# Products with the values in tied pairs of steps, and seven tiles for the weights, in a two-layer encoder

## The chip, the cores and the metric

The kernel runs on one core of a Trainium2 chip, in one launch. The metric is the device time of that core in microseconds (us). Five engines work in parallel, each through its own queue in order: TensorE (matmuls, PE in the profile, its weight loads PEld), VectorE (DVE), ScalarE (ACT), GpSimd (POOL) and SyncE (SP), which issues the transfers.

## The reference

An encoder of two layers over 1024 tokens of width 1024, all in float32:

```
layer 0: h += concat(MLA(u), stick_breaking(u)) @ w_out    u = rms_norm(h)
layer 1: h += band_attention(u) @ w_out                    u = rms_norm(h)
both:    h += (silu(u @ w_gate) * (u @ w_up)) @ w_down     u = rms_norm(h)
end:     rms_norm(h)
```

The two parts of layer 0's mixer, with 8 heads of 64 each, are what matters here:

```
stick:  z = q k^T / 8;  log_keep = log_sigmoid(-z) where s < t
        w = exp(log_sigmoid(z) + sum of log_keep over the keys between s and t)
        o = w @ v
latent: p = softmax(q k^T / sqrt(96), chunk-causal);  o = p @ v
```

## The kernel before, in words

Activations lie transposed, features on the 128 partitions and tokens along the row, in two halves of 512 queries. float32 products are made of three products of a high and a low part (`mm3`, lines 295 to 297); the products with the values (line 873) are taken in float32 as they are.

**Steps.** Heads are taken in four pairs. Stick-breaking goes, for each pair and query half, over blocks of 128 keys, from the last down to the first: 4 steps in the first half, 8 in the second, 48 in all. In the steps on the diagonal fewer query columns are alive (128, 256, 384, 512). A step (`sb_step`) has three parts. `scores` makes z for both heads (lines 942, 943), the minimum with a limit on VectorE (945, into a tile `zc` of the role "a"), exponential and logarithm on ScalarE, a maximum on VectorE (948), and splits the result into a high part (ScalarE) and a remainder, for head 0 on VectorE and for head 1 on GpSimd (both line 258). `weights` sums with a triangular matrix (964, 969) and adds the carry of the steps before (967), takes a new carry (ScalarE, and 972 on VectorE), subtracts (975) and takes the exponential, in place in `zc`. `outputs` makes the products with the values through `weighted`. Latent attention (`mla_attend`) has 48 steps too, from the first key block up: `scores` (1172 to 1174), the exponential into a tile of the role "a" (1175), sums of the exponentials on GpSimd or VectorE (1120), and `weighted`; after the last step of a half `soft_finish` makes the denominators (1137). The row maxima of the next half or pair (`mla_max`, 1097 on TensorE, 1099 on VectorE) go between the steps.

**Two heads side by side.** `weighted` issues two matmuls, one for each head, with 64 columns of weights each; they write the upper and the lower half of the same output tile. In the trace they are the ones with 128\*64, against 128\*128 of the others. `joined` binds an instruction to the one before it: it gets the highest priority and stands right behind it.

**Pipeline and order.** `step` keeps the parts of steps that are still to be issued. With `LAG` 2, a step's weights are issued two steps after its scores, its outputs two after that. `weave` puts projections of the next pair between the steps. The order on each engine is then made by a scheduling layer that works with priorities in program order and its own idea of when an instruction can start; only instructions tied by `joined`, and those of the feed-forward part, stand as written. Band attention (layer 1) ties its products with the values already by groups of four steps, with the argument `join` of `weighted` given by its own lag (`TOGETHER`).

**Tiles.** The mixer's temporaries come from `MIX0_TEMPS`: four tiles of 1024 columns for the role "a", three for "b", four for "c", three of 512 for "f". Scores and sums of both parts and the maxima share two double banks of PSUM (`banks`, tag "z").

Of the kernel before, what the change touches and what calls it, by code (L numbers as in the profile page):

```python
# [30 lines left out]
LAG = 2  # L31
TOP = 100000

TOGETHER = 4
G_MIX0, G_FFN0, G_MIX1, G_FFN1, G_FIN, G_CQ, G_CKV, G_N = 0, 8, 16, 24, 32, 40, 43, 45


MIX0_TEMPS = {"a": (4, 1024), "b": (3, 1024), "c": (4, 1024), "f": (3, 512)}
BAND_TEMPS = {"a": (6, 1024), "b": (2, 1024), "f": (2, 512), "bias": (3, 1280), "t": (2, 512), "y": (4, 512)}
FFN_TEMPS = {"vr": (4, 512), "vh": (3, 512), "vl": (3, 512), "s": (4, 512), "e": (8, 512), "x": (3, 512)}  # L40

# [118 lines left out]
class Trunk:  # L160
# [762 lines left out]
    def sb_step(self, p, hf, j, proj, vt, st, o_d):  # L923
        nc = self.nc
        mm = nc.tensor.matmul
        qq, kk, kl = proj
        kh, r = divmod(j, 4)
        ks = slice(r * P, (r + 1) * P)
        diag = kh == hf
        top = j == 4 * hf + 3  # L930
        c0 = r * P if diag else 0
        cs = slice(c0, HALF)
        x = {}

        def causal(t):
            nc.gpsimd.affine_select(out=t, in_=t, pattern=[[0, 2], [1, P]], compare_op=ALU.is_gt,
                                    fill=0.0, base=0, channel_multiplier=-1)

        def scores():
            z = self.banks()  # L940
            for e in range(2):
                mm(z[:, e, cs], kk[e][kh][:, ks], qq[e][hf][:, cs], start=True, stop=False)
                mm(z[:, e, cs], kl[kh][e][:, ks], qq[e][hf][:, cs], start=False, stop=True)
            zc, t = self.tmp("a"), self.tmp("b")
            nc.vector.tensor_scalar(zc[:, :, cs], z[:, :, cs], ZMAX, None, ALU.min)
            nc.scalar.activation(t[:, :, cs], zc[:, :, cs], AF.Exp)
            nc.scalar.activation(t[:, :, cs], t[:, :, cs], AF.Ln, bias=1.0)
            nc.vector.tensor_tensor(t[:, :, cs], t[:, :, cs], zc[:, :, cs], ALU.max)
            if diag:
                causal(t[:, :, c0:c0 + P])  # L950
            sh, sl = self.tmp("c", F32R), self.tmp("c", F32R)
            nc.scalar.copy(sh[:, :, cs], t[:, :, cs])
            for e in range(2):
                self.rest(("dve", "pool")[e], sl[:, e, cs], t[:, e, cs], sh[:, e, cs])
            x.update(zc=zc, sh=sh, sl=sl)

        def weights():
            if top:
                st["carry"] = self.tmp("b", F32R)
                nc.gpsimd.memset(st["carry"].bitcast(F32), 0.0)  # L960
            carry = st["carry"]
            b = self.banks()
            for e in range(2):
                mm(b[:, e, cs], self.tri, x["sh"][:, e, cs], start=True, stop=False)
            if not top:
                for e in range(2):
                    mm(b[:, e, cs], self.carry_ones, carry[:, e, cs], start=False, stop=False)
            for e in range(2):
                mm(b[:, e, cs], self.tri, x["sl"][:, e, cs], start=False, stop=True)
            if j > 0:  # L970
                nc.scalar.copy(carry[0:1, :, cs], b[0:1, :, cs])
                nc.vector.tensor_tensor(carry[32:33, :, cs], b[0:1, :, cs], carry[0:1, :, cs].bitcast(F32),
                                        ALU.subtract)
            w = x["zc"]
            nc.vector.tensor_tensor(w[:, :, cs], w[:, :, cs], b[:, :, cs], ALU.subtract)
            nc.scalar.activation(w[:, :, cs], w[:, :, cs], AF.Exp)
            if diag:
                causal(w[:, :, c0:c0 + P])

        def outputs():  # L980
            if top:
                st["o"] = self.out_bank()
                mm(st["o"], self.zeros, self.masks, start=True, stop=False)
            self.weighted(st["o"], vt, j, x["zc"], cs, False, j == 0)
            if j == 0:
                ot = self.tmp("f")
                nc.scalar.copy(ot, st["o"])
                nc.sync.dma_start(o_d[hf][4 + p], ot)

        idle = [lambda: None] * (LAG - 1)  # L990
        self.step(scores, *idle, weights, *idle, outputs)

# [106 lines left out]
        self.neg_max_rows(m2, hf + 1, [qs[e][hf][0][96:100, :] for e in range(2)])  # L1101
        yield

    def soft_step(self, lag, scores, cs, st, vt, j, first, last, dest):
        x = {}

        def front():
            ex = x["ex"] = self.tmp("a")
            scores(ex)
            if first:  # L1110
                st["ex"] = ex
            else:
                old = st["ex"]
                if "esum" not in st:
                    st["esum"] = self.tmp("b")
                    if cs.start:
                        self.nc.scalar.copy(st["esum"][:, :, 0:cs.start], old[:, :, 0:cs.start])
                else:
                    old = st["esum"]
                self.eng("dve" if dest[2] else "pool").tensor_tensor(st["esum"][:, :, cs], old[:, :, cs], ex[:, :, cs],  # L1120
                                                                     ALU.add)

        def back():
            if first:
                st["o"] = self.out_bank()
            self.weighted(st["o"], vt, j, x["ex"], cs, first, last)
            if last:
                self.soft_finish(st["o"], st["esum"], *dest)

        self.step(front, *[lambda: None] * (lag - 1), back)  # L1130
# [23 lines left out]
    def mla_attend(self, p, hf, proj, vt, o_d):  # L1154
        nc = self.nc
        mm = nc.tensor.matmul
        qs, ks = proj
        st = {}
        nj = 4 * hf + 4
        for j in range(nj):  # L1160
            kh, r = divmod(j, 4)
            bs = slice(r * P, (r + 1) * P)
            diag = kh == hf
            cs = slice(r * P if diag else 0, HALF)
            kr = 104 if diag else 100

            def scores(ex, kh=kh, bs=bs, cs=cs, kr=kr):
                z = self.banks()
                for e in range(2):
                    qh, ql = qs[e][hf]  # L1170
                    kth, ktl = ks[e][kh]
                    mm(z[:, e, cs], kth[0:kr, bs], qh[0:kr, cs], start=True, stop=False)  # L1172
                    mm(z[:, e, cs], kth[0:96, bs], ql[0:96, cs], start=False, stop=False)
                    mm(z[:, e, cs], ktl[0:96, bs], qh[0:96, cs], start=False, stop=True)
                nc.scalar.activation(ex[:, :, cs], z[:, :, cs], AF.Exp, scale=96 ** -0.5)

            self.soft_step(2 * LAG, scores, cs, st, vt, j, j == 0, j == nj - 1, (o_d[hf], p, p == 3))
            yield 1.0 if not diag else 1.0 - 0.25 * r


# [56 lines left out]
    def band_attend(self, p, hf, proj, tk, vt, o_d):  # L1237
# [5 lines left out]
        for n, j in enumerate(order):  # L1243
# [14 lines left out]

            self.soft_step(LAG + 1 + TOGETHER - 1 - n % TOGETHER, scores, cs, st, vt, j, n == 0, n == len(order) - 1, (o_d[hf], p, p == 7))
            yield 1.0 - 0.25 * (3 - i1 + i0)  # L1260
# [28 lines left out]
    def mixer0(self, h_d):  # L1289
# [4 lines left out]
        half = lambda hf, *e: self.out_half(hf, a["w_out0"], w_d, o_p[hf], lambda hf, m: a["x"][hf, m], ks, out, h_d, *e)  # L1294
        with self.phase("mix0", MIX0_TEMPS):
            self.load_consts()
# [250 lines left out]
```

## Time and profile before

| | |
|---|---|
| median of 3 runs | 2524.12 us (2521.48 to 2524.86) |
| profiled execution | 2524.37 us, its span 2521.8 us |
| TensorE matmuls | 2456.9 us busy, 97% of the span |
| TensorE weight loads | 1936.0 us, 77% |
| VectorE | 1849.5 us, 73% |
| ScalarE | 1156.1 us, 46% |
| GpSimd | 495.1 us, 20% |

The mean granted clock of TensorE is 0.994. Matmuls overlap in the records, so that TensorE's busy time is not its work: for what a product takes, the distance from one start to the next is read. The first mixer's attention lies between 73 and about 620 us, the band attention between about 1290 and 1820 us, the two feed-forward parts behind them.

### The profile page before, as it was taken

Reading aid. Unit: us, or ns where it says so; the run is one execution under the profiler, and the core shown is the slowest. Engines: PE = TensorE matmul, PEld = TensorE weight load, DVE = VectorE, ACT = ScalarE, POOL = GpSimd, SP = SyncE. Lnnn points to the kernel's source line nnn. Section 1 sums busy time; section 2 is a strip of 40 time slices with the busy share of each in tenths; the row PEclk is TensorE's granted clock in tenths of the full one; section 3 lists DMA queues with packets and bytes.
Section 4 is the critical chain, followed back from the end, with each engine's and each line's share of the span. In section 5 each row is a group of like instructions: output and inputs, shape, how many; then the busy total and the mean of one; then the engine's idle time right before and its main releaser. Section 6 shows DMA issues by size and latency. Waiting matters only on the chain.

```text
span 2521.8 us, 33700 instructions
## 1 busy us (share of the span) xinstructions
PE 2456.9 (97%) x11710; PEld 1936.0 (77%) x11710; DVE 1849.5 (73%) x3040; ACT 1156.1 (46%) x2004; POOL 495.1 (20%) x475
## 2 busy tenths in 40 slices
PE   8999989999999999999999999999999999999997
PEld 7766766667778888888888777776777888888886
DVE  6988897674886666677766777778688666667775
ACT  4777665444554444433253443434455444343324
POOL 0433325762000000000031334345200000000004
PEclk9999999999999999999999999999999999999998
DMA  4222102247444434576652222223853442447651
GB/s 152 58 63 62 46 21 62 61 138 234 173 140 140 146 107 145 167 260 219 207 180 70 80 88 76 76 92 124 263 174 135 145 145 102 150 160 262 219 207 71
DMA packets 192041, 341.73 MB, mean 136 GB/s; under 512 B 22400, under 2 KB 38656, under 8 KB 191872
## 3 DMA queue, kind: packets, MB, share of 16 engines
q1 hardware_dynamic: 191872, 339.59, 40.6%
q8 instruction: 92, 1.51, 0.2%
q14 instruction: 77, 0.63, 0.1%
HBM read 232.02 MB, written 92.80 MB: 129 GB/s over the span
## 4 chain that ended last, share of the span: by engine, by line
PE 74%; DVE 7%; DMA 2%; ACT 1%; issue 1%; POOL 0%; DVEq 0%; SPq 0%; POOLq 0%; ACTq 0%
PE z L77 25%; PE mm L77 14%; PE o L77 7%; PE mm L295 6%; PE mm L296 6%; PE mm L297 6%; PE o L873 3%; DVE u L77 2%; PE z L1253 1%; PE z L1254 1%; PE z L1227 1%; DVE u L318 1%; PE z L1172 1%; PE o L1137 1%; PE z L1097 1%
## 5 line engine op out<-in xcount | busy, mean ns | idle before, releaser
L77 PE MATMUL z<-u,wh 128*128 128x512 f32 x976 | 302.3, 390 | 6.4 <-DVE u L77 6.4
L77 PE MATMUL z<-u,vh 128*128 128x512 f32 x976 | 302.8, 392 | 1.9 <-DVE u L77 1.9
L295 PE MATMUL mm<-u,wh 128*128 128x512 f32 x720 | 287.6, 399 | 1.9 <-DVE f L1038 1.4
L296 PE MATMUL mm<-u,wh 128*128 128x512 f32 x720 | 283.4, 394 | 1.4 <-DVE u L258 1.4
L297 PE MATMUL mm<-u,wl 128*128 128x512 f32 x720 | 283.1, 393 | 0.0
L258 POOL TENSOR_TENSOR wl<-wr,wh 128x512 fp32r<-128x512 f32 (+2 forms) x95 | 122.5, 1293 | 775.7 <-ACT wh L253 710.4
L77 PE MATMUL mm<-u,wh 128*128 128x512 f32 x720 | 222.6, 390 | 0.0
L77 PEld LDWEIGHTS z<-u,wh 128*128 128x128 f32 x976 | 183.3, 188 | 47.3 <-DVE u L77 9.4
L77 PEld LDWEIGHTS z<-u,vh 128*128 128x128 f32 x976 | 183.7, 189 | 42.5 <-ACT u L77 2.9
L77 PE MATMUL z<-u,vl 128*128 128x512 f32 x488 | 190.4, 390 | 0.0
L77 PE MATMUL z<-u,wl 128*128 128x512 f32 x488 | 190.1, 390 | 0.0
L295 PEld LDWEIGHTS mm<-u,wh 128*128 128x128 f32 x720 | 135.3, 188 | 49.4 <-issue 22.5
L297 PEld LDWEIGHTS mm<-u,wl 128*128 128x128 f32 x720 | 135.4, 188 | 29.1 <-issue 1.7
L77 PEld LDWEIGHTS mm<-u,wh 128*128 128x128 f32 x720 | 135.2, 188 | 29.4 <-issue 1.0
L296 PEld LDWEIGHTS mm<-u,wh 128*128 128x128 f32 x720 | 135.5, 188 | 27.0 <-DVE u L258 2.0
L77 PE MATMUL mm<-u,vh 128*128 128x512 f32 x496 | 152.7, 389 | 0.0
L258 POOL TENSOR_TENSOR u<-wr,u 128x512 fp32r<-128x512 f32 x8 | 10.9, 1375 | 661.1 <-ACT u L253 661.1
L77 PE MATMUL mm<-u,wl 128*128 128x512 f32 x360 | 140.1, 389 | 0.0
L873 PE MATMUL o<-a,u 128*64 128x512 f32 (+3 forms) x768 | 139.2, 474 | 0.5 <-DVE f L1145 0.4
L1120 POOL TENSOR_TENSOR b<-b,a 128x512 f32<-128x512 f32 (+3 forms) x80 | 109.3, 1367 | 122.9 <-ACT a L1256 99.4
L77 ACT CAST wh<-wr 128x512 fp32r<-128x512 f32 (+1 forms) x190 | 110.5, 584 | 49.4 <-DVE wr L77 29.3
L77 ACT CAST vh<-vr 128x512 fp32r<-128x512 f32 (+1 forms) x166 | 95.9, 578 | 81.3 <-DVE vr L77 31.5
(244 smaller groups left out, 5815.7 us busy)
## 6 DMA issues: line engine op xcount, KB each, us to landing
u<-f_t SPq DMA_DIRECT2D x144, 256.0 KB, 5.0
vr<-in_w_up SPq DMA_DIRECT2D x88, 256.0 KB, 4.4
wr<-in_w_gate SPq DMA_DIRECT2D x88, 256.0 KB, 3.7
f_t<-x SPq DMA_DIRECT2D x72, 256.0 KB, 2.0
wr<-in_w_out SPq DMA_DIRECT2D x64, 256.0 KB, 4.0
f_t<-e SPq DMA_DIRECT2D x54, 256.0 KB, 3.5
ld<-f SPq DMA_DIRECT2D x54, 256.0 KB, 5.1
u<-u SPq DMA_DIRECT2D x96, 128.0 KB, 2.2
```

What stands on the lines that cost most here:

```text
L77: return lambda *a, **k: self.tc.keep_in_program_order(f(*a, **k))
L258: self.eng(eng).tensor_tensor(lo, src, hi.bitcast(F32), ALU.subtract)
L295: mm(out, wh, xh, start=first, stop=False, skip_group_check=onto)
L296: mm(out, wh, xl, start=False, stop=False, skip_group_check=onto)
L297: mm(out, wl, xh, start=False, stop=last, skip_group_check=onto)
L318: self.eng(eng).tensor_tensor(acc, acc, sq, ALU.add)
L873: return self.nc.tensor.matmul(o[rh, cs], vt[j // 4][:, j % 4, rh], w[:, e, cs], start=first, stop=last)
L1097: nc.tensor.matmul(z[:, e, :n], qs[e][hf][0][0:kr, r * P:(r + 1) * P], ks[e][kh][0][0:kr, :n], start=True, stop=True)
L1120: self.eng("dve" if dest[2] else "pool").tensor_tensor(st["esum"][:, :, cs], old[:, :, cs], ex[:, :, cs], ALU.add)
L1137: return nc.tensor.matmul(den[64 * e:64 * e + 64, :], self.ones[:, 0:64], esum[:, e, :], start=True, stop=True)
L1172: mm(z[:, e, cs], kth[0:kr, bs], qh[0:kr, cs], start=True, stop=False)
L1227: nc.tensor.matmul(z[:, e, :n], qs[e][hf][0][:, r * P:(r + 1) * P], ks[e][kh][0][:, k0:k0 + n], start=True, stop=True)
```

## The change

A constant `MLA_TOGETHER = 2` and an argument `join` for `soft_step`. In stick-breaking, the first step of each two issues its outputs one step later, together with the second's, and the second's product of head 0 is tied to the first's product of head 1. In latent attention the same is done for steps j and j + 1. The role "a" gets seven tiles in place of four, 12 KB more on each partition.

```diff
-MIX0_TEMPS = {"a": (4, 1024), "b": (3, 1024), "c": (4, 1024), "f": (3, 512)}
+MLA_TOGETHER = 2
+MIX0_TEMPS = {"a": (7, 1024), "b": (3, 1024), "c": (4, 1024), "f": (3, 512)}
...
+        second = (4 * hf + 3 - j) % 2 > 0
...
-            self.weighted(st["o"], vt, j, x["zc"], cs, False, j == 0)
+            self.weighted(st["o"], vt, j, x["zc"], cs, False, j == 0, second)
...
-        self.step(scores, *idle, weights, *idle, outputs)
+        self.step(scores, *idle, weights, *idle, *[lambda: None] * (not second), outputs)
...
-    def soft_step(self, lag, scores, cs, st, vt, j, first, last, dest):
+    def soft_step(self, lag, scores, cs, st, vt, j, first, last, dest, join=False):
...
-            self.weighted(st["o"], vt, j, x["ex"], cs, first, last)
+            self.weighted(st["o"], vt, j, x["ex"], cs, first, last, join)
...
-            self.soft_step(2 * LAG, scores, cs, st, vt, j, j == 0, j == nj - 1, (o_d[hf], p, p == 3))
+            self.soft_step(2 * LAG + MLA_TOGETHER - 1 - j % MLA_TOGETHER, scores, cs, st, vt, j, j == 0, j == nj - 1, (o_d[hf], p, p == 3), j % MLA_TOGETHER > 0)
```

Lines of the changed kernel behind the first edits stand two or three further down: 873 is 875 there, 948 is 951, 1097 is 1100.

On TensorE, at the start of stick-breaking, the kernel before has two products with the values (o), the sums (964 to 969), the next scores and three projection products between them:

```order
L873 MATMUL o_921<-a_768,u_575 64x128 x2
L964 MATMUL z_925<-c_849,masks 128x384 x2
L967 MATMUL z_925<-b_825,masks 128x384 x2
L969 MATMUL z_925<-c_850,masks 128x384 x2
L942 MATMUL z_937<-u_725,u_735 128x128
L943 MATMUL z_937<-u_725,u_737 128x128
L942 MATMUL z_937<-u_726,u_736 128x128
L943 MATMUL z_937<-u_726,u_738 128x128
L295 MATMUL mm_902<-u_587,wh_788 128x512
L296 MATMUL mm_902<-u_588,wh_788 128x512
L297 MATMUL mm_902<-u_587,wl_789 128x512
L873 MATMUL o_921<-a_804,u_575 64x256 x2
```

In the changed kernel the same two stand together, at the place of the second:

```order
L299 MATMUL mm_902<-u_587,wl_789 128x512
L986 MATMUL o_953<-masks 128x512
L875 MATMUL o_953<-a_768,u_575 64x128 x2
L875 MATMUL o_953<-a_804,u_575 64x256 x2
L297 MATMUL mm_902<-u_608,wh_788 128x512
L298 MATMUL mm_902<-u_609,wh_788 128x512
```

The first product moved behind the sums, the scores and the projections; one run of half-column matmuls is left of two.

On VectorE, in the second half of the first pair, the remainder for head 0 (c) was followed by the next step's full-width maximum (948); names carry their numbers here:

```order
L975 TENSOR_TENSOR a210_1191<-a210_1191,z241_1339 128x1024
L258 TENSOR_TENSOR c237_1296<-b235_1290,c236_1295 128x512
L948 TENSOR_TENSOR b244_1356<-b244_1356,a243_1355 128x1024
L255 CAST wh257_1444<-wr256_1442 128x512
L255 CAST wh303_1675<-wr302_1673 128x512
```

In the changed kernel the carry's remainder (975, 972 before) and the subtraction (978) stand between the two:

```order
L260 TENSOR_TENSOR c237_1294<-b235_1288,c236_1293 128x512
L975 TENSOR_TENSOR b181_1018<-z241_1339,b181_1018 1x1024
L978 TENSOR_TENSOR a210_1191<-a210_1191,z241_1339 128x1024
L951 TENSOR_TENSOR b244_1356<-b244_1356,a243_1355 128x1024
L260 TENSOR_TENSOR wl255_1437<-wr253_1434,wh254_1436 128x512
```

The remainder moved ahead of the carry and the subtraction, and the maximum behind both.

On TensorE in latent attention, second pair, second half, a product with the values stood between a maximum's scores (1097, z915) and the next step's scores (z917):

```order
L1174 MATMUL z914_4516<-u814_4105,u770_3914 128x256
L1097 MATMUL z915_4525<-u840_4214,u874_4346 128x384
L1097 MATMUL z915_4525<-u843_4222,u894_4432 128x384
L873 MATMUL o905_4479<-a900_4460,u699_3610 64x512 x2
L1172 MATMUL z917_4532<-u793_4013,u766_3905 128x128
```

In the changed kernel two projection products stand there:

```order
L1177 MATMUL z914_4514<-u814_4105,u770_3914 128x256
L1100 MATMUL z915_4523<-u840_4212,u874_4346 128x384
L1100 MATMUL z915_4523<-u843_4220,u894_4430 128x384
L297 MATMUL mm928_4574<-u647_3430,wh926_4570 128x512
L298 MATMUL mm928_4574<-u648_3431,wh926_4570 128x512
L1175 MATMUL z917_4532<-u792_4010,u766_3905 128x128
```

The product with the values moved one step ahead, to its partner; the projection products came forward.

## Rows read from the trace of the kernel before

**Rows 1.** The page, its first line.
```profile
span 2521.8 us, 33700 instructions
```

**Rows 2.** Busy time by stretch; columns in the first line.
```profile
core 0: us, PE busy (x) PEld busy (x) DVE busy (x) ACT busy (x) POOL busy (x), PEclk, DMA share, GB/s
73.00:95.00 22.00, 21.44 (x106) 14.85 (x105) 19.79 (x27) 15.52 (x25) 10.52 (x16) 1.00 0.28 75
95.00:146.00 51.00, 49.51 (x262) 35.79 (x261) 48.51 (x59) 38.55 (x55) 17.49 (x19) 1.00 0.19 54
146.00:167.00 21.00, 19.80 (x98) 14.08 (x99) 16.64 (x23) 14.08 (x23) 10.54 (x16) 1.00 0.23 61
167.00:218.00 51.00, 49.52 (x260) 35.97 (x260) 48.29 (x57) 38.19 (x54) 16.16 (x18) 1.00 0.22 60
239.00:302.00 63.00, 61.44 (x270) 43.45 (x271) 54.55 (x64) 41.81 (x54) 20.21 (x23) 1.00 0.20 58
302.00:334.00 32.00, 32.00 (x150) 23.88 (x149) 22.53 (x32) 20.33 (x32) 9.90 (x15) 1.00 0.10 32
334.00:360.00 26.00, 26.00 (x114) 19.54 (x115) 24.56 (x32) 18.34 (x26) 5.75 (x6) 1.00 0.07 20
360.00:386.00 26.00, 16.99 (x60) 11.01 (x57) 25.54 (x32) 14.44 (x24) 10.09 (x7) 0.80 0.11 33
...
420.00:620.00 200.00, 198.12 (x930) 130.88 (x929) 128.51 (x167) 87.14 (x136) 113.34 (x79) 1.00 0.39 125
```

**Rows 3.** TensorE in order of time, a lone step's products; start, length, instruction.
```profile
127.06 0.39 PE L297 MATMUL mm<-u,wl 128*128 128x512 f32 x1
127.38 1.08 PE L873 MATMUL o<-a,u 128*64 128x512 f32 x4
128.39 0.50 PE L295 MATMUL mm<-u,wh 128*128 128x512 f32 x1
128.72 0.39 PE L296 MATMUL mm<-u,wh 128*128 128x512 f32 x1
```

**Rows 4.** The same in band attention, four tied steps and the denominators.
```profile
1383.92 0.39 PE L297 MATMUL mm<-u,wl 128*128 128x512 f32 x1
...
1384.60 0.39 PE L297 MATMUL mm<-u,wl 128*128 128x512 f32 x1
1384.92 2.37 PE L873 MATMUL o<-a,u 128*64 128x512 f32 x16
1387.13 1.03 PE L1137 MATMUL o<-b,ones 128*64 128x512 f32 x4
1388.08 0.44 PE L1253 MATMUL z<-u,u 128*128 128x384 f32 x1
```

**Rows 5.** TensorE's waits in 73 to 330; total, times, longest.
```profile
PE z L969 <- POOL c L258: 3.0, 4, 1.1
...
PE z L969 <- DVE c L258: 0.8, 2, 0.5
```

**Rows 6.** VectorE's maxima (ns: shortest, median, longest) and one place in time.
```profile
L948 DVE TENSOR_TENSOR b<-b,a x45: 419/1212/2312, 77.0 to 392.2; 128x1024 f32<-128x1024 f32 x24, 128x256 f32<-128x256 f32 x7, 128x512 f32<-128x512 f32 x7, 128x768 f32<-128x768 f32 x7
...
195.66 0.69 DVE L258 TENSOR_TENSOR c<-b,c 128x512 fp32r<-128x512 f32 x1
196.27 2.31 DVE L948 TENSOR_TENSOR b<-b,a 128x1024 f32<-128x1024 f32 x1
```

**Rows 7.** Latent attention in order of time, from one step's scores to the next.
```profile
448.31 0.28 PE L1174 MATMUL z<-u,u 96*128 96x256 f32 x1
...
448.43 0.52 PE L1097 MATMUL z<-u,u 104*128 104x384 f32 x2
448.69 0.60 ACT L1175 ACTIVATE a<-z 128x512 f32<-128x512 f32 x1 [1.35 <-PE z L1174]
...
448.98 0.96 DVE L1099 TENSOR_REDUCE m<-z 128x2 f32<-128x768 f32 x1 [1.58 <-PE z L1097]
449.88 0.33 PE L1172 MATMUL z<-u,u 104*128 104x128 f32 x1
```

## The prediction

> **What bounds the kernel now.** I read the page first, for the span of 2521.8 us [rows 1]. Then the windows over the one stage that the change touches, the first mixer, 73 to about 620 us; the column to compare is TensorE's busy time against VectorE's [rows 2]. The stick-breaking part is eight stretches, one per head pair and query half. In the first halves (73 to 95, 146 to 167, 218 to 239, 302 to 334) TensorE is busy 19.8 to 32.0 us and VectorE clearly less, 16.64 to 22.53. In the second halves both are full: 49.51 and 48.51 us of 51 in 95 to 146, 49.52 and 48.29 in 167 to 218. From 334 to 386 VectorE has 24.56 of 26 and 25.54 of 26 us, and TensorE only 16.99 of 26 in the last stretch, at a granted clock of 0.80. In latent attention, 420 to 620, TensorE has 198.12 of 200 us and VectorE 128.51. So a shorter TensorE queue is worth its whole length in some stretches and little in others.
>
> **What a switch costs.** A product with the values is two matmuls that each use half of the array's columns (128*64), side by side. Alone in the stream of full products, such a pair of 512 columns takes from the product before it, at 127.06, to the second one after it, at 128.72: 1.66 us [rows 3]. Full products run at 0.227 us each (three from 1383.92 to 1384.60) [rows 4], so two of them are 0.45, and the lone pair costs 1.21. The band stage already ties such pairs: from 1384.92 to the first full product at 1388.08, four of 512, 384, 256 and 128 columns and the denominator's pair of 512 take 3.16 us [rows 4]. The lone one takes 1.01 over the same ends (127.38 to 128.39), so 1280 more columns cost 2.15 us, 1.68 ns a column, and a tied pair of 512 costs 0.86. Entering and leaving half-column work therefore costs 1.21 - 0.86 = 0.35 us, and that goes for each run that merges with its neighbour.
>
> **How many go.** Counted in the order of the two kernels, unbroken runs of half-column matmuls fall from 117 to 85. Stick-breaking has 48 steps, each a run of its own before; 29 runs now, not 24, since five of its pairs have other products between their two steps (so the tie isn't kept everywhere). The other 13 go in latent attention, where some denominators that followed their last product directly now stand alone; the count has that in it. 32 x 0.35 = 11.2 us, all on TensorE. No arithmetic goes or comes: each engine has as many instructions as before. From the last product with the values of latent attention on, TensorE's order is the same; nothing is expected there but the shift.
>
> **Where it lands, stretch by stretch.**
> First halves of stick-breaking: two runs fewer in each, 8 x 0.35 = 2.8 us. VectorE has 1.6 to 9.5 us less work than TensorE there. But the last product of the carry sum waits for GpSimd's half of the remainder, 3.0 us in four waits, longest 1.1 [rows 5]; in two of the four stretches TensorE arrives early and only waits longer. I take 2.4.
> Second halves: 4, 3, 2 and 2 runs fewer. Here VectorE must follow. Its work there is fixed, 48.51 us in 95 to 146, so the bounds are nothing and the full 0.35 a run. What tips it is the new order on VectorE. Its half of the remainder (0.69 us at 195.66) is followed at once by a full-width maximum with two SBUF inputs, and that one took 2.31 us, while the median of that line is 1.21 [rows 6]. Twice in the stage this stands so and costs 1.1 us, in 95 to 146 and in 167 to 218; in the new order the carry's remainder, with one input from PSUM, stands between them at both places. So VectorE gets some 1.1 us of room where it binds. I take 1.1 of 1.4, 0.9 of 1.05, 0.5 of 0.7, and in 334 to 386, where VectorE has under 2 us of idle time in 52 and TensorE waits for the latent norms, 0.2 of 0.7. Sum 2.7.
> The Trainium skill has a rule for this, in "SBUF — State Buffer", section "Who interferes with whom": a VectorE instruction with two SBUF inputs contends with a GpSimd instruction that reads SBUF, and the one that comes second is blocked, not slowed. The 2.31 us agree with that. By the rule the new order also pays where the remainder is now followed by another subtraction with two SBUF inputs (three places): 3.3 us at the same 1.1 each against 2.2 won, so the second halves would give about 1 us less.
> Latent attention: 13 x 0.35 = 4.55 us. Against it: two banks of scores alternate, and a lone product between two score groups used to give the exponential and the maximum time to empty them. In the row example the last score product starts at 448.31 and its exponential ends at 449.29 (448.69 + 0.60); the next scores can't start sooner in that bank, and before the product with the values kept TensorE busy to 449.88 [rows 7]. With the pairs, every second such gap holds two projection products in place of it: 448.43 + 2 x 0.17 + 2 x 0.227 = 449.23, 0.06 us short. The maximum of 768 elements ends at 449.94, just when TensorE would want its bank. Eight places like this at 0 to 0.25 us; I take 0.1, near what these rows give: 0.8 us lost, 3.75 left.
> The seven tiles: a weights tile of the pair's first step now lives five steps in place of four, and four tiles would have stopped the fifth step's minimum; with seven nothing waits for a tile. Before, the fourth tile was released by a product that stood ahead of the scores that need it, so it cost nothing then, and I give the two spare tiles nothing (bounds 0 to 1 us gained). The pair's first product now waits for the second's weights, and behind it on TensorE stand scores and projections; but the second product keeps its distance of four steps, so its weights are as old as before: 0, with 0.5 us lost as the other bound. The mixer's temporaries grow by 12 KB a partition and the feed-forward tiles lie over others: its first loads can wait for the last weights tiles. They overlay temporaries of the same stage before, too: 0 to 1 us, I take 0.
> Sum: 2.4 + 2.7 + 3.75 = 8.85 us. The profiled execution is 2524.37 us (its span 2521.8 and 2.6 around it), 0.25 over the median of the runs, 2524.12. 2524.37 - 8.85 = 2515.5 us.
>
> **Rivals.**
> All of it: 11.2 us, perhaps a little more with VectorE's 2.2; 2511 to 2513.2 us. For it: the second halves had TensorE fuller than VectorE, and the two collisions go. Against it: 334 to 386, where the chain of norms runs on VectorE.
> Stick-breaking pinned by VectorE: the queue there is remade by the scheduler, its work is the same, and TensorE's gain turns into waits for the remainder and the carry. Then only 302 to 334 (0.7, TensorE busy 32.00 of 32 us) and latent attention (3.75) are left, 4.45 us: 2519.9. For it: 48.51 of 51 us. "Perfetto Trace Analysis" in the Trainium skill, section "Identifying the Most-Contended Engine", says to judge VectorE by its occupancy and TensorE by its weight loads; by that rule VectorE (95%) and not TensorE (35.79 of 51 us, 70%) is the engine that binds in 95 to 146. Against it: 16.64 of 21 us in the first halves, and TensorE waited only 0.8 us for VectorE's half of the remainder in all of 73 to 330 [rows 5].
> Slower: the collision of the full-width maximum with GpSimd's half becomes the rule in place of the exception. There are 24 such maxima; 1.1 us each is 26 us, which with 8.85 saved gives 2542. It decides from eight new collisions on in the full stretches. For it: TensorE's earlier arrival moves the two engines against each other, and 2 of 24 collide already. Against it: the printed order puts another instruction between them more often than before.
>
> **How the numbers follow.** Forecast 0.52, its own range 2513 to 2519; all of it 0.20; pinned 0.23; slower 0.05. A difference of 0.2%, 5.05 us, is about what a measurement of this kernel can tell from none, so faster means under 2519.07. That holds all of the forecast and of the second case: 0.72; the pinned case is within it: 0.23; slower 0.05. The range, 2511 to 2521, takes in the full case, the pinned one and the bounds of the tiles and of the layout, and leaves out the slower one and part of the edges.
>
> **What would show it.** The half-column products of the first mixer in pairs, each pair of 512 columns with 0.86 us between its two starts, and 85 runs in the whole trace. The stage from the first product with the values to the last (73 to 620 us) shorter by 8 to 9 us, and everything behind it of the same length. No maximum of 2.31 us left on VectorE. Stretches 95 to 146 and 167 to 218 about 1 us shorter at VectorE's occupancy of 95% or more. In latent attention short new waits of scores for the exponential, under 0.25 us each. Wrong would be: TensorE's waits in 73 to 330 grown by some 5 us (pinned), a longer stretch at a clock of one half around 375 us, or a feed-forward stage that starts late.

## The result, and the profile after

The changed kernel takes 2528.75 us (median of 12 runs, 2525.29 to 2531.31), the kernel before 2523.34 in the same comparison (12 runs, 2519.27 to 2524.86): ratio 1.0021, 95% interval 1.0013 to 1.0028. It is 5.4 us slower; 8.85 us less had been forecast. The first line of its page answers to [rows 1]:

```profile
span 2528.6 us, 33696 instructions
```

The switches did go. On TensorE in order of time (start, length, instruction), two tied steps in the second half of the first head pair, which answers to [rows 3]:

```profile
126.16 0.44 PE L298 MATMUL mm<-u,wh 128*128 128x512 f32 x1
126.53 1.94 PE L875 MATMUL o<-a,u 128*64 128x512 f32 x8
128.40 0.50 PE L299 MATMUL mm<-u,wl 128*128 128x512 f32 x1
128.73 0.40 PE L297 MATMUL mm<-u,wh 128*128 128x512 f32 x1
```

From 126.16 to 128.73 is 2.57 us; less two full products at 0.227 that is 2.12 for both steps, against 2 x 1.21 = 2.42 for two lone ones: 0.30 us saved, near the 0.35 that was priced. The busy time by stretch (columns in the first line) answers to [rows 2]:

```profile
core 0: us, PE busy (x) PEld busy (x) DVE busy (x) ACT busy (x) POOL busy (x), PEclk, DMA share, GB/s
...
95.00:146.00 51.00, 47.55 (x259) 35.81 (x259) 48.16 (x56) 37.56 (x53) 17.38 (x19) 1.00 0.17 50
...
167.00:218.00 51.00, 47.14 (x249) 35.20 (x248) 45.80 (x52) 34.76 (x50) 14.95 (x18) 0.97 0.21 60
...
420.00:620.00 200.00, 195.64 (x924) 131.52 (x922) 130.58 (x165) 85.68 (x134) 114.76 (x80) 0.98 0.39 122
```

TensorE is idle where it was not: 3.45 us in 95 to 146 in place of 1.49, 3.86 in 167 to 218 in place of 1.48, 4.36 in 420 to 620 in place of 1.88, and in two of these stretches the granted clock is now below 1. The stretches are fixed in time, so they show where it idles, not how long a stage is. Its waits in 73 to 330 (total, times, longest) answer to [rows 5]:

```profile
PE z L967 <- DVE a L978: 4.4, 5, 2.0
PE z L972 <- DVE c L260: 3.3, 7, 0.8
PE z L972 <- POOL c L260: 2.6, 5, 1.1
PE o L875 <- POOL a L939: 1.4, 1, 1.4
```

With five smaller ones that is 13.7 us, against 7.2 before: 6.5 us more, where the prediction had named some 5 as a sign of being wrong. L967 is the first of the sums. It waits for L978, the subtraction on VectorE that empties the double bank of the sums of the step before; this wait was 1.3 us. L972, the last sum, waits for the remainders of both heads, 5.9 us where it was 3.8.

For the stages, distances between starts of TensorE's products were taken from the traces: stick-breaking from its first score product to step 48's, latent attention from its first score product to the last product with the values. "Tiles alone" below has the order of the kernel before. (Between the two stages lies a wait of TensorE that differs by 1 to 2 us from run to run of one order; it is left out of both.)

| kernel | half-column runs | stick-breaking, us | latent, us |
|---|---|---|---|
| tiles alone | 117 | 309.92 | 201.5 |
| changed kernel | 85 | +4.3 | +2.1 |
| stick-breaking alone | 98 | +3.2 | 0.0 |
| latent alone | 104 | -0.1 | +0.6 |
| stick-breaking's first halves | 109 | -0.6 | -1.3 |
| latent, pairs 1 and 2 | 111 | -0.1 | -2.3 |
| latent, chosen | 109 | -0.1 | -3.8 |
| three steps, untied | 116 | -0.4 | -3.0 |
| three steps, tied | 94 | -1.7 | -3.0 |
| three steps, latent chosen | 110 | -0.9 | -4.7 |

The two parts of the changed kernel are 6.4 us longer together; its profiled execution, 2530.52 us, is 7.7 above that of the tiles alone (2522.79). How far one execution can be trusted differs by stage. In stick-breaking the untied order repeats within 0.3 us (309.8 to 310.1). The tied order took 313.1 us twice and 314.2 in the changed kernel: the 1.1 us more lie behind one wait of 2.0 us at about 207 us, where in this execution alone the granted clock then stood at 0.50 for 3.4 us. The cost of the ties there is thus +3.2, not +4.3. In latent attention the first twelve steps differ by up to 1.4 us between executions of one order (the whole -1.3 of "stick-breaking's first halves" lies there, with the order of the tiles alone), and the changed kernel and "latent alone", which have one order there, differ by 1.5. So less than 1.5 us in the last column says nothing. By the executions without the extra half clock and with it, the two parts cost 3.8 to 5.3 us, of 5.4 between the medians.

### The profile page after: what moved, and what is told of

Same layout as the page of the kernel before. It is cut to its first block, busy times and chain, and to the rows that moved or that the text cites. A ratio compares the mean times of both kernels' runs of the same rounds, so it can differ in the third digit from the quotient of the medians.

```text
span 2528.6 us, 33696 instructions
## 1 busy us (share of the span) xinstructions
PE 2453.8 (97%) x11710; PEld 1941.6 (77%) x11710; DVE 1858.3 (73%) x3040; ACT 1155.7 (46%) x2004; POOL 497.0 (20%) x475
## 4 chain that ended last, share of the span: by engine, by line
PE 75%; DVE 7%; DMA 1%; issue 1%; ACT 1%; POOL 0%; DVEq 0%; SPq 0%; POOLq 0%; ACTq 0%
PE z L79 25%; PE mm L79 15%; PE o L79 7%; PE mm L297 6%; PE mm L298 6%; PE mm L299 6%; PE o L875 3%; PE z L1256 1%; DVE u L79 1%; PE z L1257 1%; PE z L1230 1%; DVE u L320 1%; PE z L1175 1%; PE o L1140 1%; PE z L1176 1%
## 5 line engine op out<-in xcount | busy, mean ns | idle before, releaser
L875 PE MATMUL o<-a,u 128*64 128x512 f32 (+3 forms) x768 | 133.6, 476 | 4.5 <-DVE f L1148 3.0
```

Source lines behind the costliest of these rows:

```text
L875: return self.nc.tensor.matmul(o[rh, cs], vt[j // 4][:, j % 4, rh], w[:, e, cs], start=first, stop=last)
```

## The experiments

Each was timed beside the kernel before; behind the ratio stands its 95% interval.

**The tiles by themselves.**

```diff
-MIX0_TEMPS = {"a": (4, 1024), "b": (3, 1024), "c": (4, 1024), "f": (3, 512)}
+MIX0_TEMPS = {"a": (7, 1024), "b": (3, 1024), "c": (4, 1024), "f": (3, 512)}
```

> The kernel before with seven tiles of the role a and nothing else; every engine's order is the same. Theory 1 (the loss comes from the new order alone): the time of before, within 1.5 us of 2523. Theory 2 (it comes from the larger temporaries, which lay the feed-forward tiles and the heap elsewhere): 2 to 5 us slower, and the stretch behind 620 us longer.

Measured: 2523.51 against 2524.02 us, ratio 0.9999 (0.9990 to 1.0007). The order on every engine is the same as before. The tiles and the layout cost nothing that can be told.

**Stick-breaking's ties alone, latent attention's alone.** From the changed kernel:

```diff
-MLA_TOGETHER = 2
+MLA_TOGETHER = 1
```

> Seven tiles, pairs tied in stick-breaking alone (98 half-column runs in place of 117). Theory 1 (its 19 removed switches, 6.7 us, come back as waits for the sums of the remade VectorE queue, and more): 1 to 3 us slower than before, with the stretch from 73 to 420 us longer by that. Theory 2 (the whole loss of the changed kernel is one blocked place in latent attention): 3 to 6 us faster. Theory 3 (pinned by VectorE): within 1 us.

Measured: 2528.06 us, 1.0012 (1.0004 to 1.0021). Nineteen switches went (6.7 us at 0.35), and stick-breaking became 3.2 us longer. Its waits in 73 to 301 are those of the changed kernel shown above within 0.2 us (4.5 for L978, 3.3 and 2.6 for the remainders). Those of the tiles alone in the same stretch:

```profile
PE z L969 <- POOL c L258: 2.8, 4, 1.1
PE z L964 <- DVE a L975: 1.3, 2, 0.7
PE z L942 <- DVE a L945: 1.2, 3, 0.4
PE z L967 <- DVE b L972: 0.9, 1, 0.9
PE z L969 <- DVE c L258: 0.8, 2, 0.5
```

The sums of all waits are 14.0 and 7.0 us. Over all of stick-breaking TensorE's idle time in the profile grew from 9.4 to 17.1 us: 7.7 more, less 6.7 of switches, is 1.0 of the 3.2. The other 2.2 would follow if the nineteen were worth 4.5 us in all, an estimate of 0.24 each, near the 0.26 of the band stage below. VectorE's busy time over the same steps grew from 271.8 to 276.0 us though its instructions are the same. Its remainders of projections (shortest, median, longest in ns; tiles alone, then stick-breaking alone):

```profile
L258 DVE TENSOR_TENSOR u<-u,u x18: 675/690/886, 72.7 to 255.2; 64x512 fp32r<-64x512 f32 x12, 128x512 fp32r<-128x512 f32 x6
```

```profile
L260 DVE TENSOR_TENSOR u<-u,u x18: 675/692/1784, 73.3 to 252.5; 64x512 fp32r<-64x512 f32 x12, 128x512 fp32r<-128x512 f32 x6
```

The median stays, single ones take 1.78 us. The collision with GpSimd went from the maximum to other instructions. The longest wait for L978 shows both what stands in front of it and such a collision (TensorE, then VectorE, start, length, instruction; stick-breaking alone):

```profile
201.27 0.73 PE L972 MATMUL z<-c,masks 128*128 128x512 f32 x2
...
207.41 0.70 PE L967 MATMUL z<-c,masks 128*128 128x512 f32 x2 [2.00 <-DVE a L978]
```

```profile
201.14 1.84 DVE L257 CAST wh<-wr 128x512 fp32r<-128x512 f32 x2
202.91 0.68 DVE L260 TENSOR_TENSOR wl<-wr,wh 128x512 fp32r<-128x512 f32 x1
203.51 0.68 DVE L260 TENSOR_TENSOR c<-b,c 128x512 fp32r<-128x512 f32 x1
204.11 0.68 DVE L260 TENSOR_TENSOR wl<-wr,wh 128x512 fp32r<-128x512 f32 x1
204.82 1.21 DVE L975 TENSOR_TENSOR b<-z,b 1x1024 fp32r<-1x1024 f32 x1
206.05 1.22 DVE L978 TENSOR_TENSOR a<-a,z 128x1024 f32<-128x1024 f32 x1
```

The sums end at 202.0. VectorE then has no pause, but it does two casts (the first 1.50 us, beside a subtraction of GpSimd), the remainders of two weights, the remainder of another step and that of the carry before it subtracts, and TensorE waits for the bank. The bank is late because other work stands ahead of its release in VectorE's queue.

Latent attention's ties alone, again from the changed kernel:

```diff
-        second = (4 * hf + 3 - j) % 2 > 0
+        second = True
...
-            self.weighted(st["o"], vt, j, x["zc"], cs, False, j == 0, second)
+            self.weighted(st["o"], vt, j, x["zc"], cs, False, j == 0)
```

> Seven tiles, pairs tied in latent attention alone (104 runs). Theory 1: up to the last first half of queries 3 to 4 us are gained; if VectorE's subtraction for the output loads is again blocked behind GpSimd's at the flush of that half (one of 3 us in place of 0.7, TensorE idle some 3 us, a stretch at half clock), 2 to 3 us slower than before in sum, and if not, 3 us faster. Theory 2 (latent ties gain nothing anywhere): the time of before without such a block.

Measured: 2523.40 us, 0.9997 (0.9988 to 1.0006). Thirteen switches went, and the stage is 0.6 us longer. By blocks of 12 steps the distances are +0.2, -1.4, +0.4 and +1.3 us. The loss sits at one place, where the third head pair hands over to the fourth: counted from the stage's first scores, those of step 40 come 2.3 us earlier than with the tiles alone, and those of step 41 come 2.2 us later. In the changed kernel, which has the same order in this stage, the place is at about 546 us. It does this on VectorE and on GpSimd (start, length, instruction):

```profile
542.97 4.70 DVE L260 TENSOR_TENSOR u<-ld,u 128x512 fp32r<-128x512 f32 x2
547.70 0.70 DVE L1147 SCALAR_TENSOR_TENSOR o<-o,f 128x512 f32<-128x512 f32 x1
548.31 0.76 DVE L1123 TENSOR_TENSOR b<-b,a 128x256 f32<-128x256 f32 x1
549.00 0.68 DVE L1148 SCALAR_TENSOR_TENSOR f<-o,f 128x512 f32<-128x512 f32 x1
```

```profile
542.42 1.76 POOL L260 TENSOR_TENSOR u<-c,u 96x512 fp32r<-96x512 f32 x1 [1.00 <-ACT u L255]
544.14 1.30 POOL L260 TENSOR_TENSOR u<-ld,u 128x512 fp32r<-128x512 f32 x1
545.82 1.31 POOL L260 TENSOR_TENSOR u<-ld,u 128x512 fp32r<-128x512 f32 x1 [0.37 <-ACT u L255]
```

Two remainders (the splits of the loaded stick-breaking outputs) last 4.70 us together, beside three subtractions of GpSimd; in the kernel before the two at this place took 1.48 and 1.16 us. Behind them stand the divisions of `soft_finish` (1147, 1148), which free the output bank. TensorE needs that bank for the four products of the next half:

```profile
546.38 0.39 PE L299 MATMUL mm<-u,wl 128*128 128x512 f32 x1
549.73 4.54 PE L875 MATMUL o<-a,u 128*64 128x512 f32 x16 [2.96 <-DVE f L1148]
554.05 1.69 PE L1140 MATMUL o<-b,ones 128*64 128x512 f32 x4
```

It waits 2.96 us, and during the wait, at 548.6, the granted clock is halved for 6.8 us (PEclk, the third number from the end, is 0.50, so 1.2 GHz):

```profile
548.60:555.40 6.80, 5.67 (x20) 2.14 (x20) 3.68 (x6) 0.00 (x0) 0.20 (x1) 0.50 0.61 207
```

The same block in the kernel before:

```profile
546.68 2.37 PE L873 MATMUL o<-a,u 128*64 128x512 f32 x16 [0.39 <-DVE f L1145]
548.85 1.06 PE L1137 MATMUL o<-b,ones 128*64 128x512 f32 x4
```

It took 2.37 us after a wait of 0.39; now it takes 4.54 after 2.96. With latent attention's ties alone the wait is 2.96 us too, the half clock lasts 3.4 us and the block takes 3.70: with the denominators behind it, that is the 1.5 us between the two runs in this stage.

**Moving the splits off that place.** In the changed kernel, the splits of the loads on VectorE alone:

```diff
-                self.split(t, hi, lo, "act", "pool" if k % 2 else "dve")
+                self.split(t, hi, lo, "act", "pool" if k % 2 and self.temps is not MIX0_TEMPS else "dve")
```

> The changed kernel with the first mixer's output loads split on VectorE alone, none on GpSimd. Theory 1 (the blocked subtraction at about 543 us costs TensorE 3 us of idle time and then 3 us at half clock): the wait of the four tied products at about 547 us falls under 1 us and the time is 4 to 6 us below the changed kernel, some 2523. Theory 2 (the lock is incidental, the denominator's chain is late anyway): within 1 us of the changed kernel, 2528.

Measured: 2529.71 us, 1.0027 (1.0018 to 1.0035): a miss. The 3.0 us for L1148 became 1.9, but a new wait of 3.0 us (scores for an exponential) and a new stretch at half clock (575 to 582 us) came in the last eight steps, and the latent stage is 4.3 us longer than with the tiles alone. The opposite, with ties in latent attention alone and both splits on GpSimd:

```diff
-                self.split(t, hi, lo, "act", "pool" if k % 2 else "dve")
+                self.split(t, hi, lo, "act", "pool" if k % 2 or self.temps is MIX0_TEMPS else "dve")
```

> As the run with ties in latent attention alone, but with the output loads of this mixer split on GpSimd alone, so that no such subtraction stands on VectorE ahead of the denominator's chain. Theory 1 (the subtraction that was blocked for 3 us delayed that chain): the wait of the four products for the last multiplication falls from 3.0 us to under 1, no half clock behind it, and the time is 3 to 5 us below that run, some 3 us below before. Theory 2 (the chain is late for other reasons): within 1 us of that run.

Measured: 2521.27 us against 2524.57, 0.9988 (0.9979 to 0.9996). The wait for L1148 is gone, and the stage is 2.2 us shorter than with the tiles alone, 2.8 shorter than with the same ties and the old splits. That fits the splits having held it, as do the 1.9 us that stayed with all of them on VectorE. But in both runs the scheduler remade the order of every engine around that place, so the splits are not the only thing that changed.

**Ties in latent pairs 1 and 2 only.**

```diff
+            tied = MLA_TOGETHER if p < 2 else 1
-            self.soft_step(2 * LAG + MLA_TOGETHER - 1 - j % MLA_TOGETHER, scores, cs, st, vt, j, j == 0, j == nj - 1, (o_d[hf], p, p == 3), j % MLA_TOGETHER > 0)
+            self.soft_step(2 * LAG + tied - 1 - j % tied, scores, cs, st, vt, j, j == 0, j == nj - 1, (o_d[hf], p, p == 3), j % tied > 0)
```

> Seven tiles, pairs tied in latent attention for the first two head pairs alone (111 runs). Theory 1 (the ties gain 0.35 us a run less some tenths, and the loss is one place at the change from the third head pair to the fourth): 1.5 to 2 us faster than before, no wait of 3 us at about 546 us. Theory 2 (the new waits for the exponentials and maxima take all): the time of before.

Measured: 2519.35 us, 0.9982 (0.9973 to 0.9991). Six runs fewer, 2.1 us at 0.35, and the stage is 2.3 us shorter. Its steps 13 to 36 are 2.5 us shorter, and 2.5 to 2.6 in each later run that has these ties. All of TensorE's waits in 420 to 620:

```profile
PE mm L298 <- DVE u L260: 1.2, 1, 1.2
PE o L875 <- DVE f L1147: 0.4, 1, 0.4
```

**Stick-breaking's first halves only.** Latent attention untied, and:

```diff
-            self.weighted(st["o"], vt, j, x["zc"], cs, False, j == 0, second)
+            self.weighted(st["o"], vt, j, x["zc"], cs, False, j == 0, second and hf == 0)
...
-        self.step(scores, *idle, weights, *idle, *[lambda: None] * (not second), outputs)
+        self.step(scores, *idle, weights, *idle, *[lambda: None] * (not second and hf == 0), outputs)
```

> Seven tiles, pairs tied in the first query halves of stick-breaking alone (109 half-column runs in place of 117). Theory 1 (in the second halves VectorE binds, and its remade queue brings subtractions and casts that stand blocked beside GpSimd; the first halves have room): 2 to 3 us faster than before, the second halves as long as before. Theory 2 (any remaking of the order costs more than the switches give): 1 us slower or more.

Measured: 2523.32 us, 0.9997 (0.9988 to 1.0007). Stick-breaking is 0.6 us shorter, of 2.8 for eight switches. The four first halves are 3.1 us shorter (0.84, 1.20, 0.77 and 0.27) and the second halves, whose code is that of before, 2.4 us longer; but part of both is work that moved: of each pair five matmuls (two steps' products with the values and the one that clears their bank) now start behind the boundary between the halves.

**Is the price of a switch real where the ties already stood?** The kernel before, with band attention tied by twos:

```diff
-TOGETHER = 4
+TOGETHER = 2
```

> The kernel before with band attention tied by two steps in place of four: 141 half-column runs in place of 117, all 24 in the band stage, with the same arithmetic. The price of a switch by itself: at 0.35 us each, 8.4 us slower (7 to 10) if TensorE binds there throughout; under 3 us if most of a switch hides in waits there.

Measured: 2524.42 us, 0.9997 (0.9988 to 1.0007), with 55 runs in band attention in place of 31. Its waits in 1290 to 1790, of the kernel before and of this one:

```profile
PE z L1253 <- DVE a L1255: 7.3, 6, 1.2
PE z L1227 <- DVE m L1230: 2.3, 4, 1.0
```

```profile
PE z L1253 <- DVE a L1255: 1.2, 6, 0.2
PE z L1227 <- DVE m L1230: 1.1, 2, 0.7
```

24 more switches are 8.4 us by the price above, and the stage is as long: from the first product of line 1253 to the last 450.51 us, against 450.17 and 450.52 in two executions of the order before (the kernel before and the tiles alone). The same six waits of scores for the bank emptied on VectorE shrink from 1.2 to 0.2 us each. TensorE's idle time between those products falls from 10.6 to 4.3 us, 0.26 a switch: a switch does cost TensorE time, somewhat less than 0.35 here, and is paid out of waits.

**Is it VectorE's load?** The kernel before with both heads' remainders on GpSimd, and the same with stick-breaking's ties and seven tiles:

```diff
-                self.rest(("dve", "pool")[e], sl[:, e, cs], t[:, e, cs], sh[:, e, cs])
+                self.rest("pool", sl[:, e, cs], t[:, e, cs], sh[:, e, cs])
```

> The kernel before with both heads' remainders in stick-breaking on GpSimd (head 0's moves off VectorE: some 40 subtractions, 30 us less on VectorE between 73 and 373 us, 60 more on GpSimd). It is the base for the next run. If VectorE binds the second halves, these get shorter, by 1 us or more each; if the step's own chain binds, they get longer, since the remainders come later.

> The same with pairs tied in stick-breaking (95 half-column runs in place of 117) and seven tiles. Theory 1 (the ties' gain was lost because VectorE, at 95% and with new blocked instructions, could not follow): with VectorE relieved the ties pay, 4 to 7 us faster than the run before this one. Theory 2 (a lone product was cover for the step's chain of scores, exponential, logarithm and remainder, whichever engine is loaded): no faster than that run, within 2 us or slower.

Measured: 2530.28 us, 1.0023 (1.0014 to 1.0033), and 2526.98, 1.0012 (1.0001 to 1.0022), both against 2524.61. VectorE is relieved to 183.85 of 227 us in 73 to 300 untied and 180.52 tied (203.38 with the tiles alone). Waits in 73 to 301, untied, then tied:

```profile
PE z L969 <- POOL c L258: 11.6, 15, 1.3
```

```profile
PE z L972 <- POOL c L260: 11.8, 18, 1.7
PE z L967 <- DVE a L978: 2.2, 4, 0.6
PE z L970 <- DVE b L975: 2.2, 2, 1.1
```

Stick-breaking takes 316.35 us untied and 315.33 tied: 22 switches (7.7 us) bring 1.0 us, with VectorE at 81% and 80%. So relieving VectorE doesn't bring the gain; but GpSimd's half became a new wait of the same kind, so this alone doesn't tell what held the gain back before.

**Is it the distance from scores to weights?** One more step between them in stick-breaking, with tiles that fit (a 6, b 3, c 6, f 2), untied and tied:

```diff
-        self.step(scores, *idle, weights, *idle, outputs)
+        self.step(scores, *idle, lambda: None, weights, *idle, outputs)
```

```diff
+        self.step(scores, *idle, lambda: None, weights, *idle, *[lambda: None] * (not second), outputs)
```

> The kernel before with one more step between a stick-breaking step's scores and its weights (three in place of two), six tiles for the role a, six for c, two for f; products with the values one by one (48 lone runs in stick-breaking). If the step's own chain (minimum, exponential, logarithm, maximum, split, remainder) sets the second halves, the added step gives it room: TensorE's waits in stick-breaking fall from about 14 us to under 8, and stick-breaking's 48 steps take 304 to 308 us in place of 309.9. If VectorE's queue sets them (272 of 310 us busy, and blocked behind GpSimd), the depth changes nothing: 309 to 311 us.

> The same with stick-breaking's products with the values tied by pairs (26 runs in place of 48, 22 x 0.35 = 7.7 us of switches less). If a lone product was only cover for a chain that came too late, the chain has room now and the ties pay: 5 to 7 us less in stick-breaking than without them at the same depth. If VectorE's queue binds, they pay 0 to 1 us, as with both remainders on GpSimd.

Measured: 2518.97 us, 0.9981 (0.9972 to 0.9989), and 2522.03, 0.9990 (0.9982 to 0.9999), both against 2523.90. Waits in 73 to 301, untied, then tied:

```profile
PE z L967 <- DVE a L978: 6.2, 7, 1.7
PE o L875 <- POOL a L939: 1.5, 1, 1.5
PE z L945 <- DVE a L978: 1.2, 1, 1.2
PE z L970 <- DVE b L975: 0.7, 2, 0.5
```

```profile
PE z L967 <- DVE a L978: 10.6, 10, 2.0
PE z L970 <- DVE b L975: 2.4, 3, 1.7
PE z L967 <- DVE a L948: 1.4, 2, 1.2
PE z L945 <- DVE a L948: 1.2, 3, 0.6
```

The waits for a remainder (3.6 us with the tiles alone, 5.9 with ties) are gone altogether: the added step does cover the chain of exponential, logarithm, split and remainder. Stick-breaking is hardly shorter for it (309.49 us), and 22 ties bring 1.25 us, not the 5 to 7 of the first theory. What is left, and grows with the ties from 9.0 to 15.6 us, are waits for VectorE to empty a double bank (L978, L948) and to make the carry (L975). They go from one step's sums to the next step's, and a step added between scores and weights gives that way no more time: sums, carry on ScalarE, its remainder on VectorE, subtraction on VectorE, bank free. But most of the time on it goes to other work. In the tied kernel 1.3 to 6.3 us lie between the end of the sums and the start of the subtraction in the ten waits for L978, 41 us together; in nine of them VectorE does work of other steps or of projections there, some 27 us. Before the wait that ends at 168.84 the sums end at 163.2 and the subtraction starts at 168.0, and VectorE does not pause: a maximum of 1.23 us, two remainders of projections (0.68 and 0.80), the carry's remainder (0.68) and the remainder of another step, which takes 1.72 us beside GpSimd's. This is read from the trace; no run put the subtraction further ahead in the queue. Collisions alone don't explain it: from untied to tied VectorE's busy time over these steps grows by only 0.6 us (273.7 to 274.3), and still 6.4 of 7.7 us are lost. One thing stays open: by the two stages the tied kernel should be 1.3 us faster than the untied one, and its median is 3.1 us slower. In the two profiled executions (2519.66 and 2520.15 us) the passage between the two stages is 2.0 us longer in the tied one, but it differs by that much between runs of one order.

**Versions that beat both.** Ties in latent pairs 1 and 2 and the second half of pair 4; the same with stick-breaking's first halves; the same with the untied three steps. Against the two latent pairs:

```diff
-            tied = MLA_TOGETHER if p < 2 else 1
+            tied = MLA_TOGETHER if p < 2 or p == 3 and hf else 1
```

> Ties in latent attention where the earlier runs gained: the first two head pairs and the last half of the fourth; none in stick-breaking (109 runs). By the stretches of the earlier runs, 2.3 us from the first two pairs and 1.6 from the last half: 3 to 4.5 us faster than before, the last half 1.6 us shorter. If the gain of the last half hung on the wait ahead of it, 2 to 2.5 us.

> Ties where they paid: the first halves of stick-breaking and, in latent attention, pairs 1, 2 and the second half of pair 4; 101 runs. If the parts add, 0.6 + 3.2 us less than with the tiles alone: 2520.2 at a time of 2524 for the kernel before, ratio 0.9985. If an earlier arrival in latent attention undoes it, as the last half of pair 3 did in the changed kernel, 2522 to 2524.

> Stick-breaking with three steps between scores and weights, untied (as deep_untied), and ties in latent attention in pairs 1, 2 and the second half of pair 4 alone; 110 runs. If ties pay in latent attention at any state of the rest, 2 to 3 us less than deep_untied (0.9981): 2516 to 2517 at a time of 2524 for the kernel before, ratio 0.997. If they only took back what the deeper order has already given in latent attention's first steps (3.0 us less in the first twelve), 0 to 1 us less.

Measured: 2519.89 against 2524.61 us, 0.9986 (0.9977 to 0.9995); 2520.59 against 2523.90, 0.9986 (0.9977 to 0.9995); 2518.10 against 2526.03, 0.9968 (0.9957 to 0.9979). The first halves add nothing to the chosen latent ties. The last half's tie adds 0.7 us in its own steps and nothing that the medians show. The three steps with the chosen ties are the fastest kernel here, though the interval overlaps with that of the three steps untied (0.9972 to 0.9989). Its latent stage is 1.7 us shorter than that of the same kernel untied: the first twelve steps lose 1.7 of what the deeper order had given them, the others win 3.4. It is the one version whose whole interval lies beyond 0.2%.

## Why the prediction was wrong, point by point

- **The price of a switch and their number**: right in kind, with the price some way too high: 0.30 us in the tied pair shown above and 0.26 on average in the band stage, for 0.35; 85 runs.
- **That a switch taken out of TensorE's stream is time won**: this step failed, and with it the sign. It was argued from TensorE being fuller than VectorE in the second halves. A lone product lies between one group of sums or scores and the next, and VectorE works towards emptying a bank meanwhile. Without it the time returned as waits for L978 and the remainders (+7.7 us of idle time for 6.7 us of switches), and stick-breaking became 3.2 us longer where 5.1 shorter had been forecast. The bounds for the second halves were nothing and the full 0.35 a run, so a loss stood outside them. The band experiment shows the same from the other side, at equal length. Why the bank comes late is read from the trace: its release stands behind other work in VectorE's queue. The pinned rival named the waits for the remainder and the carry, but let them take the gain and no more.
- **First halves, 2.4**: with these ties alone stick-breaking as a whole became 0.6 us shorter. The 3.1 of the first halves and the 2.4 lost in the second are in part work that moved across the boundary.
- **Second halves, 2.7**: they became 8.3 us longer in the changed kernel; part of that is work that moved in from the first halves, eleven projection products and eleven matmuls into the output banks (the fourth first half alone is 3.5 us shorter). The argument was one pair of instructions at two places: the two maxima of 2.31 us [rows 6] did go from there. But the queue was remade everywhere, and by the rule that I had cited from the Trainium skill, "SBUF — State Buffer", section "Who interferes with whom", the price moved to other subtractions with two SBUF inputs: 1.78 us for 0.69. The trace agrees with the rule, each beside a subtraction of GpSimd. Two casts took 1.5 us for 0.42 in the same way; they have one input, and the rule as I cited it does not cover them. I priced it at two places that vanish and, as a rival, at three that appear, and the whole was 4.2 us of busy time.
- **Occupancy as the measure**: the rule of "Perfetto Trace Analysis" in the Trainium skill, section "Identifying the Most-Contended Engine", would have made VectorE the bound, and the rival built on it (2519.9 us) came nearer than mine, still with the wrong sign. But with VectorE relieved to 81% the ties brought 1.0 of 7.7 us, with GpSimd's half as the new wait; and the rows of the deeper pipeline point at the order of VectorE's queue rather than its load.
- **Latent attention, 3.75**: none of the short waits of scores for the exponential that were priced at 0.8 us shows among TensorE's waits, and pairs 1, 2 and the last half gave 3.8 us where they alone were tied (0.5 of it in the first twelve steps, which repeat no better than 1.4). What I had put at nothing without looking was the output bank at 546 us: 2.96 us of wait, some 2.2 us of half clock in the block and 0.6 in the denominators behind it.
- **The pair's first product waiting for the second's weights, 0 to 0.5**: one wait of 1.4 us for a masked weight (L939), beyond the bound.
- **Seven tiles, layout, everything behind the mixer, 0**: right as far as these runs can tell. The ratio with the tiles alone is 0.9999; behind latent attention's last product with the values the changed kernel's profiled execution takes 1909 us, and those of all the others 1906 to 1911.
- **The slower rival** had a collision of the maximum as the rule. One maximum in the changed kernel takes 2.32 us in stick-breaking, where none was forecast; the mechanism was of the right kind, and on the wrong instruction. It had the sign by a cost of 26 us; VectorE's busy time grew by 4.2.

## What to carry to other kernels

Time taken out of a full engine's stream counts only if the next thing that it waits for is already early; before pricing a removal, look what the removed piece stood in front of, and when the bank or tile that comes next was freed. Where each step of a recurrence passes through another engine's queue, packing work into pairs takes the filler from between the steps, so do it only where the trace shows no such wait near (here latent pairs 1 and 2). When such a wait is there, look which instructions stand ahead of the release in the other engine's queue. And when a scheduler remakes a queue, count every pair of neighbours that can collide, not the ones that were seen colliding before.

## What was not expected of the hardware

One VectorE subtraction can be held by several of GpSimd's in a row: two that took 1.48 and 1.16 us before took 4.70 us together beside three of 1.76, 1.30 and 1.31 us, the first of them 3.02 beside two of GpSimd's. And a wait of 2.96 us went with 6.8 us at a granted clock of 0.50, in which a block of half-column products took 4.54 us in place of 2.37: with the denominators the wait cost nearly twice its length. The same order can come off otherwise: in another execution the same wait went with 3.4 us at 0.50 and a block of 3.70. And one wait of 2.0 us, the same in three executions, was followed by 3.4 us at 0.50 in one of them and by a full clock in the other two.
